# Weight halves split into high and low part by two transfers instead of by ScalarE and VectorE

## The chip, the core and the metric

The kernel runs on one core of one Trainium2 chip. The core has a matrix engine (TensorE, in the profile PE, its weight loads PEld), two elementwise engines (VectorE, in the profile DVE, and ScalarE, in the profile ACT), a third one that also issues transfers (GpSimd, POOL), a queue that only issues transfers (SyncE, SP) and 16 DMA engines that all queues share. The metric is the device time of one execution in microseconds (us), lower is better. A profile of one execution stands beside the timed runs.

## What is computed

One layer of a hybrid encoder block on 512 tokens of width 1024, all in float32: a normed projection into 11520 columns, three token mixers side by side (a gated short convolution, a gated linear recurrence, and a delta-rule recurrence over 16 heads in chunks of 64 tokens), their gated sum, an output projection with residual, and a squared-ReLU MLP with residual and a last norm.

```python
h = rms_norm(x, norm1_g[l])
p = h @ w_in[l]                                   # 1024 x 11520
...
m = gate_a * y_a + gate_b * y_b + gate_c * y_c
x = x + m @ w_out[l]                              # 1024 x 1024
h2 = rms_norm(x, norm2_g[l])
x = x + jnp.square(jax.nn.relu(h2 @ mlp_w1[l])) @ mlp_w2[l]   # 1024 x 4096 x 1024
return rms_norm(x, final_g)
```

## The kernel before

**Split products.** TensorE's fast 32-bit type (float32r) holds fewer bits than float32. So every large operand is split into a high part (the value rounded to float32r) and a low part (the value minus the high part, also float32r), and each product is made of three matmuls, high by high, high by low and low by high (`mm3`, L153 to L155). The activations are split on the chip when they are made (`hh` and `hl`, `h2h` and `h2l`, `ah` and `al`).

**The weight stream.** Weights come in tiles of 128 x 1024, each used for one block of 128 output columns (or, in the second MLP product, 128 rows), and each loaded as two halves of 128 x 512 (256 KB). `load_half` (L127) makes one half: SP loads `raw` (L129, three buffers), ScalarE casts it to `whi` (L131, four buffers), VectorE subtracts to get `wlo` (L94 from L133, four buffers). A tile serves 8 x 3 = 24 matmuls. There are 170 tiles, 340 halves: 180 halves of `w_in`, 32 of `w_out` (each of its 8 tiles is loaded twice, once for each half of the tokens), 64 and 64 of the MLP.

**Stages.** The start loads x, takes its norm (squares by POOL and ScalarE at L232 and L234, their sum by TensorE, the root `rsb` on VectorE at L181) and meanwhile multiplies three tiles with x before its norm's scale; then x is scaled (L251 on POOL for five of the eight parts) and split into `hh` and `hl`. Four groups follow. In each the critical part is the delta-rule recurrence: small matrices (`amat`), a triangular inverse by elimination on VectorE (`dg` and `Z`, 62 steps), and a chain over eight chunks of small matmuls; as filler beside it run the projections of the other mixers, in an order that `weave` and the priorities fix. The output projection (`w_out`) works on half of the tokens at a time, so its matmuls have 256 columns instead of 512. Then the MLP: 32 tiles of `w1`, after each of which ScalarE takes the relu (L914) and splits the square (L922), and 32 of `w2`.

**Order and queues.** A scheduler sets the order of instructions on each engine from the order of the program and priorities; `load_w` asks for priority over what is emitted beside it. Each engine then works strictly in that order: an instruction that waits holds up all behind it, and that is so for queues of transfers too. In this kernel POOL issues some 50 transfers, of intermediate results (`mpd`, `mhd`, `mld`, `mh`, `ml`, `x2d`) and of x; SP issues all weights. POOL's own computing is the four squares and five scalings of the start, a few fills, and eight products at the very end.

Of the kernel before, what the change touches and what calls it, by code (L numbers as in the profile page):

```python
# [9 lines left out]
F32 = mybir.dt.float32  # L10
# [8 lines left out]
P = 128  # L19
# priorities of the weight stream, the prologue and the critical steps over what is emitted beside them  # L20
OFF, OFFS, OFFP = 160, 20, 30
CP, CPI, CPP = 150, 60, 30
# empty steps that leave the latency of an inverse, or of a norm, to the filler
NINV, NPOST = 16, 6
# steps of the fillers, and their shares by part of the critical path
# [63 lines left out]
def block_kernel(ctx, tc, xt, win, par, mulr, sw, wout, w1, w2, fg, cst, eyes, out):  # L89
# [3 lines left out]
    def tt(o, a, b, op):  # L93
        return v.tensor_tensor(out=o, in0=a, in1=b, op=op)  # L94
# [32 lines left out]
    def load_half(src, i):  # L127
        raw = wp.tile([P, S], F32, tag="raw", name="raw", bufs=3)
        sy.dma_start(raw, src[:, i * S:(i + 1) * S])  # L129
        hi = wp.tile([P, S], F32R, tag="whi", name="whi", bufs=4)  # L130
        ac.copy(hi, raw)  # L131
        lo = wp.tile([P, S], F32R, tag="wlo", name="wlo", bufs=4)
        tt(lo, raw, f(hi), SUB)  # L133
        return hi, lo
# [22 lines left out]
    def pin(first, mm):  # L157
        # in the order of the program, behind the matmuls before it
        if first:
            tc.keep_in_program_order(mm)  # L160

    def rsqrt(x, y, t):
        # Newton's steps from a first guess on the exponent; within 2 ulp after the third
# [6 lines left out]
    def rsqrt_rows(pool, o, ps, low, scale=1.0):  # L170
        # rows alike in each 32: tokens to partitions, the root there, and back
# [11 lines left out]
    # =======================================================================  # L183
    # projections and the three branches
    # =======================================================================
# [24 lines left out]
    wlr = [[load_half(win[CN[("lr", 0)]], 0)]]  # L210
    for a, n in ((0, 1), (1, 1), (2, 2)):
        sy.dma_start(xT[:, a:a + n], xt[a:a + n].rearrange("k p t -> p k t"))
    wlr[0].append(load_half(win[CN[("lr", 0)]], 1))
# [81 lines left out]
    # low-rank inputs, and the first key tile, on x before its norm's scale  # L295
# [10 lines left out]
    # derived per-channel values  # L306
    # sigmoid(z) = (1 + tanh(z / 2)) / 2 throughout: tanh shares its table with exp
# [30 lines left out]
    # softplus of the recurrence's parameter  # L338
# [33 lines left out]
    def krv(g, G_):  # L372
# [5 lines left out]
        for jj in range(2):  # L378
# [51 lines left out]
            # by head: the two tiles' halves side by side  # L430
# [17 lines left out]
    def amat(G_):  # L448
        # A^T = [b|k]^T [a|r], masked
# [605 lines left out]
```

## Time and profile before

| | |
|---|---|
| Median of 3 runs | 1188.13 us (1186.85 to 1191.43) |
| Profiled execution, its span | 1188.4 us |
| TensorE busy | 1155.3 us (97%) |
| VectorE busy | 786.9 us (66%) |
| ScalarE busy | 550.5 us (46%) |
| POOL busy | 59.2 us (5%) |
| Moved by DMA | 114.69 MB, mean 97 GB/s |

The profiled execution has no time of its own beside its span; it lies within the three timed runs. The profile gives for each group of instructions the source line, engine, operation, output and inputs, the count, then the busy time and the mean duration of one, and last the idle time of the engine just before them with what ended it. Matmuls overlap, so that the mean duration of one (410 ns) is longer than the distance from one to the next. The line is often that of a helper: all of VectorE's two-operand operations have L94, and the tile's name tells them apart.

### The profile page before, as it was taken

What the parts mean: (1) busy time and instruction counts of PE and PEld (TensorE: products, weight loads), DVE (VectorE), ACT (ScalarE), POOL (GpSimd) and SP (SyncE); (2) the same over time, 40 slices, a digit from 0 to 9 for tenths busy, and PEclk for the clock granted to TensorE, in tenths of its full rate; (3) what the DMA queues carried; (4) which work ended last, traced back from release to release, by engine and by line L of the source; (5) the groups of instructions that cost most, each with busy time, mean ns of one, the idle gap of its engine ahead of it and who ended that gap; (6) DMA issues with size and microseconds to landing.
All of it is one profiled execution on the core that took longest, in us unless ns stands there. A gap on an engine that the chain in (4) does not pass through costs nothing.

```text
span 1188.4 us, 17270 instructions
## 1 busy us (share of the span) xinstructions
PE 1155.3 (97%) x6396; PEld 896.6 (75%) x6396; DVE 786.9 (66%) x1537; ACT 550.5 (46%) x1005; POOL 59.2 (5%) x99
## 2 busy tenths in 40 slices
PE   8999989999999999989999989999999999999996
PEld 4677876677777677767677766889888888888885
DVE  7997985689975678985688975677544444222225
ACT  6655364444556443565444545556444443222224
POOL 4100000000000000000000011000000000000003
PEclk9899988999999999999999999999999999999999
DMA  5231230222332122233122244436323333433322
GB/s 183 89 89 54 89 98 28 63 85 71 96 114 72 41 80 80 85 106 90 46 80 67 71 126 150 151 116 187 124 90 98 89 98 118 154 101 91 105 89 98
DMA packets 61973, 114.69 MB, mean 97 GB/s; under 512 B 7232, under 2 KB 10816, under 8 KB 61888
## 3 DMA queue, kind: packets, MB, share of 16 engines
q1 hardware_dynamic: 54960, 95.49, 26.2%
q0 software_dynamic: 6352, 17.30, 4.6%
q8 instruction: 50, 0.82, 0.3%
q10 hardware_dynamic: 576, 0.79, 0.2%
q14 instruction: 35, 0.29, 0.1%
HBM read 104.64 MB, written 8.91 MB: 96 GB/s over the span
## 4 chain that ended last, share of the span: by engine, by line
PE 84%; DVE 12%; issue 2%; ACT 1%; DMA 0%; SPq 0%; DVEq 0%; ACTq 0%
PE pp L153 12%; PE pp L155 11%; PE pp L154 11%; PE acc L153 6%; PE acc L154 6%; PE acc L155 6%; PE p L155 5%; PE p L153 5%; PE p L154 5%; DVE wlo L94 3%; PE py L582 2%; PE pA L458 2%; PE py L584 2%; DVE Z L94 2%; DVE dg L94 2%
## 5 line engine op out<-in xcount | busy, mean ns | idle before, releaser
L94 DVE TENSOR_TENSOR wlo<-raw,whi 128x512 fp32r<-128x512 f32 x340 | 235.4, 695 | 250.6 <-ACT whi L131 241.7
L131 ACT CAST whi<-raw 128x512 fp32r<-128x512 f32 x340 | 209.7, 619 | 379.1 <-PE acc L155 124.5
L155 PE MATMUL pp<-hh,wlo 128*128 128x512 f32 x696 | 284.4, 410 | 14.8 <-DVE wlo L94 14.5
L153 PE MATMUL pp<-hh,whi 128*128 128x512 f32 x696 | 285.0, 412 | 1.3 <-ACT hh L254 1.3
L154 PE MATMUL pp<-hl,whi 128*128 128x512 f32 x696 | 282.1, 407 | 3.1 <-DVE hl L97 3.1
L155 PEld LDWEIGHTS pp<-hh,wlo 128*128 128x128 f32 x696 | 133.2, 191 | 53.1 <-DVE wlo L94 21.6
L153 PEld LDWEIGHTS pp<-hh,whi 128*128 128x128 f32 x696 | 133.2, 191 | 34.6 <-issue 1.9
L154 PEld LDWEIGHTS pp<-hl,whi 128*128 128x128 f32 x696 | 133.4, 192 | 33.6 <-DVE hl L97 3.7
L155 PE MATMUL p<-h2h,wlo 128*128 128x512 f32 (+1 forms) x264 | 103.0, 390 | 0.1
L153 PE MATMUL p<-h2h,whi 128*128 128x512 f32 (+1 forms) x264 | 103.0, 390 | 0.0
L154 PE MATMUL p<-h2l,whi 128*128 128x512 f32 (+1 forms) x264 | 102.8, 389 | 0.0
L154 PE MATMUL acc<-wlo,ah 128*128 128x512 f32 x256 | 99.7, 390 | 0.0
L155 PE MATMUL acc<-whi,al 128*128 128x512 f32 x256 | 99.6, 389 | 0.0
L153 PE MATMUL acc<-whi,ah 128*128 128x512 f32 x256 | 99.6, 389 | 0.0
L155 PEld LDWEIGHTS p<-h2h,wlo 128*128 128x128 f32 x264 | 49.7, 188 | 11.6 <-DVE wlo L94 0.3
L154 PEld LDWEIGHTS p<-h2l,whi 128*128 128x128 f32 x264 | 49.7, 188 | 11.3
L153 PEld LDWEIGHTS p<-h2h,whi 128*128 128x128 f32 x264 | 49.7, 188 | 11.3
L154 PEld LDWEIGHTS acc<-wlo,ah 128*128 128x128 f32 x256 | 48.1, 188 | 10.1 <-DVE wlo L94 0.3
L153 PEld LDWEIGHTS acc<-whi,ah 128*128 128x128 f32 x256 | 48.1, 188 | 10.1
L155 PEld LDWEIGHTS acc<-whi,al 128*128 128x128 f32 x256 | 48.1, 188 | 10.0
L94 DVE TENSOR_TENSOR Z<-Z,dg 64x31 f32<-64x31 f32 (+15 forms) x124 | 42.2, 340 | 4.1
L94 DVE TENSOR_TENSOR dg<-Z 64x31 f32<-64x31 f32 (+15 forms) x124 | 42.2, 340 | 4.1
(299 smaller groups left out, 1591.3 us busy)
## 6 DMA issues: line engine op xcount, KB each, us to landing
raw<-in_win SPq DMA_DIRECT2D x180, 256.0 KB, 2.6
raw<-in_w SPq DMA_DIRECT2D x128, 256.0 KB, 2.7
raw<-in_wout SPq DMA_DIRECT2D x32, 256.0 KB, 2.6
swr<-in_sw SPq DMA_DIRECT2D x16, 128.0 KB, 2.1
x2T<-in_xt POOLq DMA_DIRECT2D x4, 512.0 KB, 7.1
x2d<-st POOLq DMA_DIRECT2D x8, 256.0 KB, 2.8
xr<-x2d POOLq DMA_DIRECT2D x1, 2048.0 KB, 8.7
xT<-in_xt SPq DMA_DIRECT2D x3, 512.0 KB, 6.8
```

The costliest lines, as they stand in the source:

```text
L94: return v.tensor_tensor(out=o, in0=a, in1=b, op=op)
L131: ac.copy(hi, raw)
L153: pe.matmul(ps, wh, xh, start=start, stop=False)
L154: pe.matmul(ps, wh, xl, start=False, stop=False)
L155: pe.matmul(ps, wl, xh, start=False, stop=stop)
L458: pe.matmul(pts[h][:, ci], G_.BK[rows, jj, c], G_.AR[rows, jj, c], start=True, stop=True)
L582: pe.matmul(o, RT[64 * h:64 * h + 64, jj, c], St[64 * h:64 * h + 64, jj], start=True, stop=False)
L584: pe.matmul(o, AXt[:, 2 * h + jj, c, 1], sv[:, 2 * h + jj], start=St is None, stop=True)
```

## The change

The changed `load_half` has no `raw` tile in the steady stream. POOL issues a transfer from float32 in memory into the float32r tile `whi`, which rounds on the way. ScalarE writes the negated high part into `wlo`. POOL issues a second transfer of the same weights that adds them to what is in `wlo`, so that `wlo` ends as the weight minus its high part. `whi` has six buffers now, `wlo` five. The two halves of the very first tile keep the old way, with `raw` in a buffer of another pool that is free then. Comments were removed from the source; the lines of the changed kernel are shifted by 7, so the matmuls of `mm3` are L160 to L162 there.

```diff
-    def load_half(src, i):
-        raw = wp.tile([P, S], F32, tag="raw", name="raw", bufs=3)
-        sy.dma_start(raw, src[:, i * S:(i + 1) * S])
-        hi = wp.tile([P, S], F32R, tag="whi", name="whi", bufs=4)
-        ac.copy(hi, raw)
-        lo = wp.tile([P, S], F32R, tag="wlo", name="wlo", bufs=4)
-        tt(lo, raw, f(hi), SUB)
+    def load_half(src, i, pool=None):
+
+        src = src[:, i * S:(i + 1) * S]
+        hi = wp.tile([P, S], F32R, tag="whi", name="whi", bufs=6)
+        lo = wp.tile([P, S], F32R, tag="wlo", name="wlo", bufs=5)
+        if pool is not None:
+            raw = pool.tile([P, S], F32, tag=("lgh", "lgl")[i], name="raw")
+            sy.dma_start(raw, src)
+            ac.copy(hi, raw)
+            tt(lo, raw, f(hi), SUB)
+            return hi, lo
+        gp.dma_start(hi, src)
+        ac.activation(lo, f(hi), AF.Copy, scale=-1.0)
+        gp.dma_start(lo, src, accum_op=ADD)
         return hi, lo
...
-    wlr = [[load_half(win[CN[("lr", 0)]], 0)]]
+    wlr = [[load_half(win[CN[("lr", 0)]], 0, sp)]]
...
-    wlr[0].append(load_half(win[CN[("lr", 0)]], 1))
+    wlr[0].append(load_half(win[CN[("lr", 0)]], 1, sp))
```

Three places show what moves. The first is the start on POOL: `sq` are the squares of x for the first norm, `xT` is x. Before:

```order
L232 TENSOR_TENSOR sq<-xT 128x512 [waits DMAHW2_49]
L232 TENSOR_TENSOR sq<-xT 128x512 [waits DMAHW4_49]
L232 TENSOR_TENSOR sq<-xT 128x512 [waits DMAHW6_49]
L925 MEMSET epst 128x1 [waits Activation_49]
L232 TENSOR_TENSOR sq<-xT 128x512 [waits DMAHW7_49]
L251 TENSOR_TENSOR xT<-xT,rsb 128x512 [waits DMAHW3_49,DVE_49,Activation_49]
```

and in the change:

```order
L138 DMA whi<-in_win 128x512 [waits PE_49]
L140 DMA wlo<-in_win 128x512 [waits Activation_49] x2
L138 DMA whi<-in_win 128x512 [waits PE_49]
L140 DMA wlo<-in_win 128x512 [waits DMASW0_49,Activation_49]
L140 DMA wlo<-in_win 128x512 [waits DMASW1_49,Activation_49]
L140 DMA wlo<-in_win 128x512 [waits DMASW2_49,Activation_49]
L239 TENSOR_TENSOR sq<-xT 128x512 [waits DMAHW7_49]
```

The fourth square, which waited for nothing but x, now stands behind six transfers of `whi` and five of `wlo`, two of the former waiting for TensorE (PE) and all of the latter for ScalarE (Activation).

The second place is the first MLP product. Before, SP's queue held the loads of `raw` and nothing else, here of `w_out` and the MLP:

```order
L129 DMA raw<-in_wout 128x512 x32
L129 DMA raw<-in_w 128x512 x128
```

In the change POOL's queue has, with the buffers' numbers (a `wlo` has the number of its `whi` plus one):

```order
L138 DMA whi_8668<-in_w1 128x512
L140 DMA wlo_8634<-in_w1 128x512
L138 DMA whi_8673<-in_w1 128x512
L140 DMA wlo_8669<-in_w1 128x512
L138 DMA whi_8708<-in_w1 128x512
L140 DMA wlo_8674<-in_w1 128x512
L138 DMA whi_8713<-in_w1 128x512
```

The adding transfer of half 8668 stands behind the casting transfer of the next half, 8673, and ahead of that of the one after, 8708.

The third place is the second pass of the output projection, again on POOL in the change; before, POOL had only the stores of `x2d` there:

```order
L865 DMA x2d<-st 128x512 x8
```

and now:

```order
L138 DMA whi_7485<-in_wout 128x512
L140 DMA wlo_7415<-in_wout 128x512
L140 DMA wlo_7448<-in_wout 128x512
L140 DMA wlo_7453<-in_wout 128x512
L138 DMA whi_7490<-in_wout 128x512
L140 DMA wlo_7486<-in_wout 128x512
L138 DMA whi_7523<-in_wout 128x512
L872 DMA x2d_69<-st_7374 128x512
L138 DMA whi_7528<-in_wout 128x512
L140 DMA wlo_7491<-in_wout 128x512
L138 DMA whi_7561<-in_wout 128x512
L140 DMA wlo_7524<-in_wout 128x512
```

Here the adding transfer of half 7490 stands behind the casting transfers of the next two, 7523 and 7528, and a store of `x2d` stands between.

## The prediction

> **What bounds the kernel now.** I read the page first (busy time, chain of waits, costliest groups), then the stretches, then the timelines of single engines. The page:
>
> ```profile
> PE 1155.3 (97%) x6396; PEld 896.6 (75%) x6396; DVE 786.9 (66%) x1537; ACT 550.5 (46%) x1005; POOL 59.2 (5%) x99
> ...
> PE 84%; DVE 12%; issue 2%; ACT 1%; DMA 0%; SPq 0%; DVEq 0%; ACTq 0%
> ...
> L94 DVE TENSOR_TENSOR wlo<-raw,whi 128x512 fp32r<-128x512 f32 x340 | 235.4, 695 | 250.6 <-ACT whi L131 241.7
> L131 ACT CAST whi<-raw 128x512 fp32r<-128x512 f32 x340 | 209.7, 619 | 379.1 <-PE acc L155 124.5
> L155 PE MATMUL pp<-hh,wlo 128*128 128x512 f32 x696 | 284.4, 410 | 14.8 <-DVE wlo L94 14.5
> ```
>
> TensorE is the bound: 97% busy, 33 us idle in 1188.4. VectorE's low parts cost 235 us of VectorE but only 14.5 us of TensorE's idle time. In stretches (columns: PE, PEld, DVE, ACT, POOL busy, clock, DMA share, GB/s):
>
> ```profile
> 0.00:50.00 50.00, 41.59 (x136) 27.55 (x136) 41.15 (x76) 31.49 (x53) 16.26 (x22) 0.93 0.45 141
> 600.00:700.00 100.00, 95.16 (x448) 73.97 (x445) 88.40 (x165) 44.07 (x74) 4.31 (x8) 0.98 0.27 83
> 900.00:1000.00 100.00, 100.00 (x429) 80.38 (x428) 47.43 (x71) 42.12 (x72) 0.00 (x0) 1.00 0.30 95
> 1100.00:1188.00 88.00, 78.88 (x348) 64.81 (x346) 30.69 (x48) 25.86 (x50) 9.26 (x7) 0.98 0.29 96
> ```
>
> Of the 33 us, 8.4 lie in the start and 9.1 in the last stretch, which the change does not reach; what VectorE could give back is the 14.5. VectorE is the bound only inside the elimination of each group; for the last one, all engines and then the wlo instructions alone:
>
> ```profile
> 645.00:692.00 47.00, 45.53 (x193) 35.54 (x192) 43.97 (x95) 21.41 (x35) 0.64 (x2) 1.00 0.26 78
> 645.00:692.00 47.00, 9.00 (x13) 1.00 0.26 78
> ```
>
> VectorE has 44 of 47 us there, 9 of them for wlo, but TensorE is at 45.5 of 47 on filler: a shorter elimination moves TensorE's work and removes little of it. TensorE's own pace, from its timeline:
>
> ```profile
> 662.14 0.40 PE L153 MATMUL pp<-hh,whi 128*128 128x512 f32 x1
> ...
> 671.98 0.40 PE L153 MATMUL pp<-hh,whi 128*128 128x512 f32 x1
> ```
>
> These are 14 rounds of three matmuls in 9.84 us: 0.234 us each. A weight tile has 24 of them, 5.63 us, so a half (256 KB) is used up every 2.81 us in the MLP and under dense filler.
>
> **The change part by part.** It removes 338 of 340 subtractions from VectorE (338 x 0.695 = 235 us). ScalarE exchanges a cast for a negation of the same shape, about 0.62 us both. SP's weight loads go to POOL, twice: 338 casting and 338 adding transfers, 676 issues. The nearest rows are a plain POOL load of 256 KB (its issue, then its landing), a run of ten such loads, and SP's load:
>
> ```profile
> L717 POOL DMA_DIRECT2D u<-mpd x6: 544/546/562, 314.7 to 728.3; - x6
> DMA to landing us min/median/max: 2.9/3.7/4.5
> ...
> DMA to landing us min/median/max: 2.9/4.8/6.0
> raw<-in_w SPq DMA_DIRECT2D x128, 256.0 KB, 2.7
> ```
>
> Issuing alone is 676 x 0.55 = 372 us of POOL, which has 59 busy: hidden. In engine time, the MLP row (share 0.30 at 95 GB/s) puts the full rate at 317 GB/s, so 256 KB cost 0.83 us. No row shows a cast or an add. I take the casting load at 0.83; the adding one lies between 0.83 (as a load) and 1.66 (a load plus a second reading of the same size). A pair is then 1.66 to 2.49 us, below 2.81: by bytes the MLP still fits.
>
> The Trainium skill speaks against the change here: "Collectives: The Full Stack", section "The bandwidth ceiling: the fold count and why AG ≠ RS ≠ AR", says that an adding DMA step runs at about half the rate of a copy, since it has to read two sources through one read ring. By that rule the adding transfer is at the upper end, 1.66 us; the terms below would be 31 us for the MLP and 22 for the output projection, and the sum 1241. No row of this trace can show it.
>
> The tighter limit is **a loop through POOL's queue**. As the order of instructions shows, whi of half n is issued, then wlo of n-1, then whi of n+1, then wlo of n; and wlo of n waits for ScalarE's negation, which waits for whi of n to land. Behind that waiting issue stands whi of n+2. So two halves take one loop: landing 3.7 + negation 0.62 + issue 0.55, and some queueing, because the previous adding transfer, issued 0.55 earlier, is ahead in the same queue (the ten loads in a row landed after 2.9 at the least, 6.0 at the most). That is 1.66 - 0.55 = 1.11 at the upper end, 0.28 with a plain load, 0.70 halfway; I take 0.83, one plain transfer, since the landings of 3.7 were had with less than half of the traffic. The loop is 5.70 us, against TensorE's 5.63 for two halves. Lower end 2.9 + 0.62 + 0.55 = 4.07, upper end 4.5 + 1.11 + 0.62 + 0.55 = 6.78.
>
> *MLP, 64 tiles.* In the second product (32 tiles) the loop misses by 0.07 x 32 = 2 us. In the first, ScalarE is also held for each tile:
>
> ```profile
> 892.52 0.59 ACT L914 ACTIVATE r<-p 128x512 f32<-128x512 f32 x1
> 893.98 0.62 ACT L922 CAST ah<-r 128x512 fp32r<-128x512 f32 x1 [0.86 <-DVE r L94]
> ```
>
> From 892.52 to 894.60 it is 2.1 of 5.63 us; a landing that falls into it (0.37 of the time) waits 1.05 on average, so 0.39 more, and (0.07 + 0.39) x 32 = 15 us. From a slot's release TensorE has five halves, 14.1 us, and the way to a landed low part takes the 5.70 and another landing, 3.7 + 0.83, 10.2 in all, so 3.9 us are in reserve: 2 + 15 - 4 = **+13**. Ends: 0 (loop at 4.07) and (6.78 - 5.63) x 64 + 12 = +86.
>
> *Output projection.* Its matmuls have half the width, so halves go fast (casts to whi, columns as before):
>
> ```profile
> 790.00:800.00 10.00, 3.63 (x7) 1.00 0.57 161
> 800.00:810.00 10.00, 2.78 (x5) 1.00 0.65 205
> 810.00:820.00 10.00, 4.31 (x7) 1.00 0.62 191
> 820.00:830.00 10.00, 3.70 (x6) 1.00 0.58 167
> ```
>
> 25 halves in 40 us, 1.6 us each, with the DMA at 0.6 already for one load per half. In the new order three whi run ahead there, so the loop gives 5.70 / 3 = 1.90, and the pair's engine time 1.66 to 2.49. I take 2.1: 25 x 0.5 = **+12**. Ends: +1 (1.66) and +22 (2.49).
>
> *Groups.* 13 halves in 47 us are 3.6 us each, and the loop gives 2.85, so the stream keeps up there and no longer waits for VectorE. Of the 14.5 us I take two thirds back: **-10**. Ends: -14.5 and 0 (ScalarE's and POOL's own waits take VectorE's place).
>
> *Start.* POOL squares four x tiles for the first norm; the fourth now stands behind six whi, two of which wait for TensorE to be done with the first tile's halves, and five wlo, which wait for ScalarE:
>
> ```profile
> 11.48 1.45 POOL L232 TENSOR_TENSOR sq<-xT 128x512 f32<-128x512 f32 x1
> ...
> 23.18 0.71 DVE L181 STREAM_TRANSPOSE rsb<-rqq 128x512 f32<-128x512 f32 x1
> 24.02 8.02 POOL L251 TENSOR_TENSOR xT<-xT,rsb 128x512 f32<-128x512 f32 x5 [11.10 <-ACT spt L343]
> ```
>
> I estimate the fourth at 20 instead of 11.5, and rsb, the norm's scale, some 8 us later; 48 matmuls on unscaled x (11.3 us) cover part. **+5**; ends 0 (all covered) and +10 (nothing covered, and POOL's five scalings interrupted by issues).
>
> *Other work in POOL's queue.* Ten loads of mh and ml and one of mab were alone there:
>
> ```profile
> 710.58 0.54 POOL L799 DMA_DIRECT2D mh<-mhd  x1 [11.93 <-ACT AXt L521]
> ...
> 716.24 0.72 POOL L801 DMA_DIRECT2D mab<-mpd  x1 [0.34 <-DMA mh<-mhd]
> ```
>
> Now weights stand behind the 6.4 us of issues and their 3.1 MB (9.9 us at 317 GB/s), against 3.9 in reserve: **+5**; ends 0 (TensorE's small matmuls of the chain cover it) and +12 (the wait for AXt counts too).
>
> Sum against the profiled execution: 1188.4 - 10 + 5 + 5 + 12 + 13 = 1213. The median run, 1188.13, is the same within 0.3. All lower ends together: 1188.4 - 14.5 + 1 = 1175; all upper ends: 1188.4 + 10 + 12 + 22 + 86 = 1318.
>
> **The rivals.** *Everything is hidden* (chance 0.21): whi lands near 2.9, the loop is 4.07, six slots of whi and five of wlo cover the rest, and the 14.5 us come back less a little at the start: 1176. For it: 11.2 to 14.1 us of lead. Against it: median POOL landings of 3.7 with less than half of the traffic. *The transfers are slow* (0.17): casting or adding costs the engines more than a row shows; it decides once a pair takes over 2.81 us. At 3.3: 128 x 0.49 = 63 in the MLP, 25 x 1.7 = 42 in the projection, and the 10 of the start and mh: about 1303. At 4.0: 152 + 60 + 10 and 4 x 13 x 0.4 = 21 in the eliminations: 1431. For it: no row shows such a transfer; against it: nothing either. *Loss and gain cancel* (0.12): loop at 5.2, the projection at 1.8, 1185 to 1192. That the subtraction does not leave VectorE is excluded by the order.
>
> **How the numbers follow.** About 0.5% (6 us) is what a measurement of this kernel can tell from no change. The forecast, 1195 to about 1265, has 0.50; faster 0.21; same 0.12; slower 0.50 + 0.17 = 0.67. The range of 8 in 10 goes from 1174, just under the hidden case, to 1325, which leaves out the worse half of the slow transfers. The forecast's own range is 1195 to 1265.
>
> **What would show it.** Right: POOL near 370 us of issues or above; VectorE down by 235; POOL waiting for ScalarE's wlo in the MLP; TensorE idle before L162 with a DMA as releaser from 790 to 830 and in the MLP; the weight transfers landing at 3.7 to 5 us. The fourth squaring near 20 us would bear out the start. Wrong: no idle time of TensorE in the MLP (hidden case), or DMA shares near 1 with landings over 8 us (slow transfers). If POOL's issue takes over 1.4 us, POOL itself sets the pace, and the loop was the wrong step.

## The result and the profile after

The changed kernel takes 1354.24 us, median of four runs (1349.96 to 1369.02), against 1187.49 us (1185.57 to 1191.43) for the kernel before: a ratio of 1.142, 95% interval 1.137 to 1.146. It is 14% slower. The forecast was 1213, its range 1174 to 1325: the direction was right, the size was not.

Three kinds of rows of the page after (busy time; chain of waits; costliest groups):

```profile
PE 1210.9 (89%) x6396; PEld 918.9 (68%) x6396; DVE 581.0 (43%) x1199; ACT 549.9 (41%) x1005; POOL 536.4 (40%) x775
...
issue 32%; PE 31%; POOL 21%; DMA 10%; ACT 3%; DVE 3%; POOLq 0%; SPq 0%; ACTq 0%; DVEq 0%
...
L139 ACT ACTIVATE wlo<-whi 128x512 fp32r<-128x512 f32 x338 | 212.6, 630 | 547.6 <-DMA whi<-in_w 192.0
...
L140 POOL DMA_DIRECT2D wlo<-in_w x128 | 110.3, 865 | 222.3 <-ACT wlo L139 212.9
...
L161 PE MATMUL acc<-wlo,ah 128*128 128x512 f32 x256 | 105.6, 413 | 30.8 <-DMA wlo<-in_w 30.7
```

VectorE's 235 us of low parts are gone, and its busy time is shorter by 206 us (581.0 instead of 786.9; some of those rows overlapped others). TensorE has fallen from 97 to 89% busy, although its busy time has grown from 1155.3 to 1210.9 us with the same 6396 matmuls. The chain that was 84% TensorE is now TensorE, POOL, DMA and issue. The third to fifth row give its links in order: ScalarE's negation waits for the casting transfer, POOL's adding transfer waits for the negation, TensorE waits for the adding transfer. No engine is the bound; a sequence of latencies is.

The same in stretches (columns: PE, PEld, DVE, ACT, POOL busy, clock, DMA share, GB/s):

```profile
0.00:50.00 50.00, 37.36 (x119) 25.00 (x120) 38.02 (x74) 27.81 (x46) 29.06 (x43) 0.93 0.78 182
600.00:700.00 100.00, 95.78 (x595) 69.22 (x596) 65.81 (x153) 41.59 (x86) 28.41 (x42) 1.00 0.53 106
900.00:1000.00 100.00, 88.92 (x413) 69.93 (x414) 21.56 (x36) 36.04 (x67) 47.29 (x69) 0.97 0.86 181
1200.00:1300.00 100.00, 88.67 (x367) 68.70 (x366) 0.00 (x0) 19.09 (x31) 42.46 (x60) 0.98 0.81 159
```

In the two stretches of the MLP (the last two rows) TensorE is busy for 88.9 and 88.7 of 100 us; before, it had 100 of 100 from 900 to 1000. Where each stage ends is read from the first and last start of the matmuls that only it has, `mh,whi` (output projection), `h2h,whi` (first MLP product), `whi,ah` (second). Before, then after:

```profile
L153 PE MATMUL acc<-mh,whi x128: 274/281/390, 757.2 to 822.0; 128*128 128x256 f32 x128
L153 PE MATMUL p<-h2h,whi x264: 277/397/483, 822.3 to 1003.7; 128*128 128x512 f32 x124, 128*128 128x256 f32 x8
L153 PE MATMUL acc<-whi,ah x256: 387/389/393, 1004.4 to 1178.0; 128*128 128x512 f32 x128
```

```profile
L160 PE MATMUL acc<-mh,whi x128: 274/282/583, 814.2 to 918.5; 128*128 128x256 f32 x128
L160 PE MATMUL p<-h2h,whi x264: 277/394/628, 911.4 to 1122.0; 128*128 128x512 f32 x124, 128*128 128x256 f32 x8
L160 PE MATMUL acc<-whi,ah x256: 387/389/632, 1122.7 to 1342.0; 128*128 128x512 f32 x128
```

The table has the same three ends for every kernel of this study, as durations in us of the profiled execution. The stages overlap a little, and an execution can differ from the median by some us, so differences under 5 us are not read. The median leaves out executions over 1.5% above the kernel's fastest: two of "every second half" (1341.5, the profiled one, and 1344.9) and one of its "groups only" (1284.5). The expectations were written with other marks for the stages (430 us for the MLP after, where the table has 423.5, and 97 for the output projection, where it has 104.3).

| kernel | to the end of the output projection | of it, to its first matmul | MLP 1 | MLP 2 | rest | median of the runs |
|---|---|---|---|---|---|---|
| before | 822.0 | 757.2 | 181.7 | 174.3 | 10.4 | 1187.5 |
| after | 918.5 | 814.2 | 203.5 | 220.0 | 12.9 | 1354.2 |
| more high buffers (7 and 4) | 860.8 | 769.9 | 185.6 | 194.9 | 12.6 | 1256.7 |
| casting alone | 863.9 | 784.0 | 182.0 | 180.9 | 12.7 | 1243.2 |
| adding alone | 874.4 | 786.4 | 186.6 | 206.3 | 11.9 | 1281.4 |
| loop cut | 824.7 | 741.0 | 181.1 | 180.2 | 13.0 | 1202.2 |
| no adding | 854.8 | 771.0 | 181.1 | 175.4 | 13.9 | 1234.1 |
| 7 and 5 buffers | 843.0 | 754.6 | 184.8 | 213.8 | 13.2 | 1259.3 |
| negated twice | 941.8 | 844.2 | 221.9 | 243.0 | 12.5 | 1429.8 |
| every second half | 922.3 | 826.3 | 195.3 | 210.8 | 11.4 | 1330.3 |
| every second half, groups only | 885.7 | 804.6 | 181.8 | 174.2 | 10.2 | 1258.1 |
| GpSimd subtracts | 851.5 | 782.2 | 182.3 | 174.3 | 10.3 | 1224.1 |
| three castings ahead | 855.3 | 768.3 | 184.4 | 184.0 | 13.0 | 1228.1 |
| three ahead, groups only | 835.3 | 753.5 | 182.3 | 175.8 | 10.6 | 1207.2 |

Of the 166.5 us between the two profiled executions, 96.5 are lost by the end of the output projection, 21.8 in the first and 45.7 in the second MLP product.

Part of this is a price that none of the edits below isolates: TensorE's granted clock. The traces show it at 1 or at 0.5; at 1 a 512-column matmul starts every 234 ns, at 0.5 every 427 ns (medians in the kernel after). Up to the end of the output projection, before and then after, followed by two stretches of that projection in the kernel after (columns as above):

```profile
0.00:822.00 822.00, 798.44 (x4818) 604.91 (x4819) 640.75 (x1314) 422.55 (x780) 46.53 (x86) 0.98 0.30 92
```

```profile
0.00:918.50 918.50, 830.17 (x4830) 628.62 (x4831) 521.07 (x1105) 423.55 (x784) 346.25 (x513) 0.94 0.69 143
819.00:842.00 23.00, 23.00 (x122) 17.84 (x120) 5.95 (x19) 6.11 (x16) 6.57 (x10) 0.50 0.68 158
845.00:868.00 23.00, 19.26 (x162) 16.39 (x162) 9.72 (x31) 8.17 (x19) 11.19 (x16) 1.00 0.79 162
```

At half clock TensorE was busy all the time and made 122 matmuls in 23 us; at full clock it made 162, with idle time between them. Up to the end of the output projection its idle time grew from 24 to 88 us and its time at half clock from 31 to 102 us. Half of the latter growth, 36 us, is the most that it can have cost; the two together, 65 + 36, cover the 96.5. Over the whole execution idle time grew by 111 us and time at half clock by 92, so up to 46 of the 166.5 us are the clock's. An estimate from the spans and mean clocks says the same: span times clock is 1289 to 1297 us in the four executions after and 1169 to 1175 before, some 120 us apart.

In the kernel after, each of the 17 stretches at half clock begins when TensorE has been idle for at least 1.3 of the 3.4 us before it; in other runs some begin without any idle time, so what sets them off is not shown. With the loop cut the clock is 0.989 again (0.985 before, 0.953 after), so this price goes with the turn; but casting alone, which has no turn, also shows 0.970. Where a run below is compared, the time at half clock is given where it is a large part of the loss.

The turn can be seen on POOL and on ScalarE in the second MLP product of the kernel after (timelines: start, duration, what, idle time before it and its releaser):

```profile
1230.63 0.84 POOL L140 DMA_DIRECT2D wlo<-in_w  x1 [4.22 <-ACT wlo L139]
1231.17 0.87 POOL L138 DMA_DIRECT2D whi<-in_w  x1
1232.52 0.85 POOL L140 DMA_DIRECT2D wlo<-in_w  x1 [0.48 <-ACT wlo L139]
1233.07 0.88 POOL L138 DMA_DIRECT2D whi<-in_w  x1
1237.27 0.85 POOL L140 DMA_DIRECT2D wlo<-in_w  x1 [3.33 <-ACT wlo L139]
...
1244.14 0.85 POOL L140 DMA_DIRECT2D wlo<-in_w  x1 [3.30 <-ACT wlo L139]
```

```profile
1236.34 0.63 ACT L139 ACTIVATE wlo<-whi 128x512 fp32r<-128x512 f32 x1 [4.11 <-DMA wlo<-in_w]
```

The high part issued at 1231.17 is negated at 1236.34, and the adding transfer that needs this goes out at 1237.27; behind it stands the next casting transfer. From one such adding transfer to the next it takes 6.64 us (1230.63 to 1237.27) and 6.87 (to 1244.14), for the two halves of one weight. The stage's mean is 220.0 / 32 = 6.88. TensorE could use them up in 5.45 (174.3 / 32, before; in the first product 181.7 / 32 = 5.68). (The releaser named on ScalarE's row, a landing of `wlo`, is long past by the order of the issues; the wait is for the casting transfer.)

### The profile page after: what moved, and what is told of

It is laid out like the page before. It is cut to its first block, busy times and chain, and to the rows that moved or that the text cites. A ratio compares the mean times of both kernels' runs of the same rounds, so it can differ in the third digit from the quotient of the medians.

```text
span 1354.9 us, 17282 instructions
## 1 busy us (share of the span) xinstructions
PE 1210.9 (89%) x6396; PEld 918.9 (68%) x6396; DVE 581.0 (43%) x1199; ACT 549.9 (41%) x1005; POOL 536.4 (40%) x775
## 4 chain that ended last, share of the span: by engine, by line
issue 32%; PE 31%; POOL 21%; DMA 10%; ACT 3%; DVE 3%; POOLq 0%; SPq 0%; ACTq 0%; DVEq 0%
POOL whi L138 12%; POOL wlo L140 9%; PE pp L162 6%; PE pp L161 5%; PE pp L160 5%; DMA whi<-in_win 4%; DMA wlo<-in_w 2%; PE py L589 2%; PE py L591 2%; DMA wlo<-in_win 1%; PE pu L557 1%; PE pT L524 1%; ACT wlo L139 1%; PE pS L574 1%; PE pu L565 1%
## 5 line engine op out<-in xcount | busy, mean ns | idle before, releaser
L139 ACT ACTIVATE wlo<-whi 128x512 fp32r<-128x512 f32 x338 | 212.6, 630 | 547.6 <-DMA whi<-in_w 192.0
L162 PE MATMUL pp<-hh,wlo 128*128 128x512 f32 x696 | 287.9, 415 | 17.8 <-DMA wlo<-in_win 17.8
L160 PE MATMUL pp<-hh,whi 128*128 128x512 f32 x696 | 283.6, 409 | 4.1 <-ACT hh L261 4.1
L140 POOL DMA_DIRECT2D wlo<-in_win x178 | 155.7, 883 | 235.2 <-ACT wlo L139 230.7
L138 POOL DMA_DIRECT2D whi<-in_win x178 | 128.4, 726 | 211.0 <-PE pp L162 143.7
L140 POOL DMA_DIRECT2D wlo<-in_w x128 | 110.3, 865 | 222.3 <-ACT wlo L139 212.9
L162 PEld LDWEIGHTS pp<-hh,wlo 128*128 128x128 f32 x696 | 133.6, 192 | 56.2 <-DMA wlo<-in_win 25.7
L160 PEld LDWEIGHTS pp<-hh,whi 128*128 128x128 f32 x696 | 134.2, 193 | 35.4 <-ACT hh L261 4.6
L161 PE MATMUL acc<-wlo,ah 128*128 128x512 f32 x256 | 105.6, 413 | 30.8 <-DMA wlo<-in_w 30.7
L162 PE MATMUL p<-h2h,wlo 128*128 128x512 f32 (+1 forms) x264 | 107.5, 408 | 12.7 <-DMA wlo<-in_w 12.1
L138 POOL DMA_DIRECT2D whi<-in_w x128 | 107.8, 847 | 9.4 <-PE acc L162 5.0
L160 PE MATMUL p<-h2h,whi 128*128 128x512 f32 (+1 forms) x264 | 103.4, 392 | 0.1
L162 PE MATMUL acc<-whi,al 128*128 128x512 f32 x256 | 102.1, 400 | 0.0
L160 PE MATMUL acc<-whi,ah 128*128 128x512 f32 x256 | 101.7, 398 | 0.0
L97 DVE SCALAR_TENSOR_TENSOR xr<-acc,sc,xr 128x512 f32<-128x512 f32 x8 | 6.0, 745 | 202.0 <-PE acc L162 202.0
L94 DVE TENSOR_TENSOR r<-r 128x512 f32<-128x512 f32 x32 | 22.2, 692 | 131.2 <-ACT r L921 131.2
L162 PEld LDWEIGHTS p<-h2h,wlo 128*128 128x128 f32 x264 | 49.9, 189 | 39.0 <-DMA wlo<-in_w 29.5
L161 PEld LDWEIGHTS p<-h2l,whi 128*128 128x128 f32 x264 | 50.1, 190 | 11.4
```

Source lines behind the costliest of these rows:

```text
L138: gp.dma_start(hi, src)
L139: ac.activation(lo, f(hi), AF.Copy, scale=-1.0)
L140: gp.dma_start(lo, src, accum_op=ADD)
L160: pe.matmul(ps, wh, xh, start=start, stop=False)
L161: pe.matmul(ps, wh, xl, start=False, stop=False)
L162: pe.matmul(ps, wl, xh, start=False, stop=stop)
```

## The experiments

Two theories stood against each other. **Loop**: what costs is the turn through POOL's queue (casting transfer lands, ScalarE negates, adding transfer goes out, next casting transfer goes out), which takes longer than TensorE takes for the halves it covers. **Bytes**: what costs is that two transfers for each half, one of them adding, fill the DMA engines. A third question came up on the way: what is left when the loop is gone.

### What a transfer costs by itself

A kernel that only moves weights: 40 plain loads of 256 KB each from SP and POOL, 40 casting ones, 40 adding ones without and 40 with a cast, then eight of each of POOL's kinds one at a time.

```diff
+    for k in range(N):                      # casting loads
+        gp.dma_start(T[k], src(k))
+    for k in range(N):                      # adding and casting
+        gp.dma_start(T[k], src(k), accum_op=add)
```

> All of the block's work is left out: 40 loads of 256 KB back to back on SP (plain), then on POOL 40 plain, 40 casting, 40 adding without a cast and 40 adding with a cast, each into 40 separate tiles, then 8 of each POOL kind into one tile, each waiting for the one before. It prices the disputed transfers by themselves. Theory L (the loop through POOL's queue: landing, negation, issue, two halves for each turn, sets the pace of the changed kernel; the engines have room): plain and casting near 0.8 us each in a row, adding at most 1.7, so a pair under 2.5 us against TensorE's 2.81 a half; one at a time a casting load lands after about 3 us. Theory D (the 16 DMA engines set the pace): casting plus adding take 3.2 us or more of the engines, as much as the 3.3 to 3.4 us a half that the MLP of the changed kernel needs.

The rate in 40 equal slices of its 316 us; then the casting and the adding transfers one at a time, each with its landing:

```profile
GB/s 221 389 388 386 389 385 389 279 387 388 383 205 205 205 204 205 204 204 243 262 211 204 204 206 153 99 67 71 95 66 82 60 62 63 66 66 66 66 66 66
```

```profile
L111 POOL DMA_DIRECT2D t<-in_w x8: 527/529/536, 219.7 to 243.2; - x8
...
DMA to landing us min/median/max: 2.8/3.1/3.3
```

```profile
L115 POOL DMA_DIRECT2D t<-in_w x8: 857/861/865, 279.5 to 308.3; - x8
...
DMA to landing us min/median/max: 3.7/3.8/4.1
```

Plain and casting loads run at the same 387 GB/s, 0.68 us for 256 KB: the cast costs the engines nothing. Adding transfers run at 205 GB/s, 1.28 us, with and without a cast. A pair is 1.95 us, well under the 2.81 us that TensorE takes for a half.

A second such kernel asks whether the prices add up when the two kinds alternate in one queue, and when compute engines work beside them.

> The block's work is left out. Four stretches of 256 KB transfers from the weights on POOL's queue: 20 plain casting ones; then 60 pairs of a casting and an adding transfer in turn, to tiles of their own; the same 60 pairs beside TensorE (8 matmuls a pair), ScalarE and VectorE; then 40 casting ones beside TensorE. Alone and unmixed the two kinds took 0.68 and 1.28 us of the DMA engines. If prices add up, a pair takes 1.95 us, 268 GB/s, in both stretches of pairs. If mixing two kinds in one queue costs (the theory of slow transfers), the first stretch of pairs shows 2.4 us or more (under 220 GB/s); if it is the engines' work that slows the transfers, only the second does.

```profile
GB/s 185 357 315 253 267 272 274 270 269 271 274 264 269 273 273 265 271 272 272 271 269 299 280 272 273 271 269 272 272 258 274 273 268 270 274 376 384 383 394 78
...
q0 software_dynamic: 43200, 78.66, 111.8%
```

Throughout the stretches of pairs it runs at some 271 GB/s, 1.94 us for a pair. The matmuls, which wait for nothing, fill only the first half of the span, so it is the first half of these slices that stands beside the engines; its rate is no lower. The prices add up. The second row is a warning for the reading of traces: the packets of one queue took 111.8% of the 16 engines' span, so packets overlap in this share and in the DMA columns. A share near 1 does not mean that no more could be moved.

### The loop cut, its bytes kept

```diff
-        ac.activation(lo, f(hi), AF.Copy, scale=-1.0)
+        ac.activation(lo, wcon, AF.Copy, scale=-1.0)
```

> The changed kernel, with one thing else: ScalarE's negation reads a constant tile in place of the high part, so that it no longer waits for the casting transfer (the low parts are then the whole weights, so the product is another; instructions, bytes and buffers are those of the changed kernel). Loop through POOL's queue: the turn is gone, MLP 360 to 385 us in place of 430, in all 1190 to 1250. Transfers fill the DMA engines: the MLP stays above 410 and the whole above 1310.

1202.19 us, ratio 1.013 (1.009 to 1.016): 152 of the 167 us are gone with one operand. Bytes, transfers, buffers and queues are the same. In POOL's order one or two castings now stand ahead of an adding transfer instead of two; the negation, and with it the adding transfer, no longer waits for them. Its page, POOL's timeline in the second MLP product, and a stretch of the first:

```profile
PE 1157.0 (97%) x6396; PEld 897.7 (75%) x6396; DVE 582.8 (49%) x1200; ACT 549.1 (46%) x1005; POOL 540.0 (45%) x775
```

```profile
1125.10 0.55 POOL L141 DMA_DIRECT2D whi<-in_w  x1 [2.52 <-PE acc L165]
...
1130.54 0.55 POOL L141 DMA_DIRECT2D whi<-in_w  x1 [2.52 <-PE acc L165]
```

```profile
900.00:1000.00 100.00, 100.00 (x429) 80.39 (x428) 24.93 (x36) 42.58 (x72) 50.64 (x72) 1.00 0.97 187
```

POOL now waits for TensorE to free a slot, and the rows come every 5.44 us: TensorE sets the pace again. The DMA share is 0.97 with TensorE at 100 of 100, more than the 0.86 of the kernel after. The theory of bytes falls here. Of the 152 us, up to 50 are time at half clock that went with the turn (129 us of it after, 30 here). Against the kernel before, the end of the output projection is 2.7 us late and the MLP 5 us. Its first matmul comes 16.2 us earlier than before, but up to 12 of these are the clock too: 7 us at half clock up to there, against 31.

### The turn made longer by a known time

```diff
         ac.activation(lo, f(hi), AF.Copy, scale=-1.0)
+        ac.activation(lo, f(hi), AF.Copy, scale=-1.0)
```

> The changed kernel with ScalarE negating each half twice (the second time over the first), 0.63 us more in every turn of POOL's queue and nothing else on it; ScalarE was busy 41% of the span. Loop: with turns of 6.6 to 6.9 us for two halves in the MLP, 64 turns there become 40 us longer, MLP 465 to 475 in place of 430; over all 169 turns at most 106 us, so 1400 to 1460 in all. Had the transfers' bytes set the time, 0.63 us of a ScalarE that has room would move it by less than 10 us: 1345 to 1365.

1429.84 us, ratio 1.201 (1.191 to 1.211), 76 us more than the change. The MLP went from 423.5 to 464.9 us, 41.4 more, where 64 turns of 0.63 give 40.3. POOL's adding transfers in the second product:

```profile
1294.43 0.86 POOL L141 DMA_DIRECT2D wlo<-in_w  x1 [4.92 <-ACT wlo L140]
...
1302.35 0.86 POOL L141 DMA_DIRECT2D wlo<-in_w  x1 [5.04 <-ACT wlo L140]
...
1309.79 0.86 POOL L141 DMA_DIRECT2D wlo<-in_w  x1 [4.57 <-ACT wlo L140]
```

7.92 and 7.44 us; the stage's mean is 243.0 / 32 = 7.59, 0.72 more than the 6.88 of the kernel after. What is added to the turn appears in the MLP's time. By products it is 18.4 us, 0.57 for each turn, in the first, where POOL's order is that of the kernel after, and 23.0 us, 0.72 each, in the second, where two and three castings stand ahead in turn. Before the MLP, 23.3 us were lost over 105 turns, 0.22 each: by this the turn would bind about a third of the time there, which one pair of profiles is too coarse to show.

### The turn made shorter by a cheaper neighbour

The second transfer casts without adding: it still waits for the negation, and only its engine time falls from 1.28 to 0.68 us.

```diff
-        gp.dma_start(lo, src, accum_op=ADD)
+        gp.dma_start(lo, src)
```

> The changed kernel, with the second transfer casting without adding (the low parts are then copies of the high ones; it still waits for the negation, so queue, loop and buffers stay, and only the engine time of a pair falls from 1.95 to 1.36 us). Loop: the turn is shorter only by what the casting transfer lands earlier, 0.5 to 1.0 us of 6.7, so MLP 375 to 410 and in all 1270 to 1325. Transfers fill the DMA engines: MLP under 370, in all under 1250.

1234.05 us, ratio 1.039 (1.025 to 1.053). Landings (count, KB each, median us from issue to landing), of the kernel after and of this one:

```profile
whi<-in_w POOLq DMA_DIRECT2D x128, 256.0 KB, 4.9
wlo<-in_w POOLq DMA_DIRECT2D x128, 256.0 KB, 4.3
```

```profile
whi<-in_w POOLq DMA_DIRECT2D x128, 256.0 KB, 3.4
```

The MLP came out at 356.5 us against 356.0 before: hidden. This is better than the loop's expectation (375 to 410) and by its numbers alone looks like the theory of bytes; with the run before, which kept all the bytes and got the time back too, it reads otherwise. The casting transfer is itself unchanged. It lands 1.5 us earlier with no adding transfer in front of it; that would bring the turn from 6.88 to about 5.4, no longer than TensorE's 5.45. I had put this shortening at 0.5 to 1.0 us. Bytes matter, but as latency within the turn.

### Buffers, and who is ahead of whom in POOL's queue

The order of instructions shows how many casting transfers are issued before an adding one waits for the first of them. In the change it is two nearly everywhere. With seven high and four low buffers it is mostly four (four and three in turn in the second MLP product), with seven and five mostly three, without any other edit.

```diff
-        hi = wp.tile([P, S], F32R, tag="whi", name="whi", bufs=6)
-        lo = wp.tile([P, S], F32R, tag="wlo", name="wlo", bufs=5)
+        hi = wp.tile([P, S], F32R, tag="whi", name="whi", bufs=7)
+        lo = wp.tile([P, S], F32R, tag="wlo", name="wlo", bufs=4)
```

> The changed kernel with seven buffers for whi and four for wlo instead of six and five, the same space. On POOL four casting transfers now stand ahead of the adding transfer of the first of them instead of two, so one turn of the loop serves four halves; bytes and transfers are the same. Theory L: a turn of 6.7 us gives 1.7 us a half, below 2.81, so the MLP (431 us in the changed kernel, 356 before) goes back to 360 to 380, the output projection (97 us, 65 before) to 75 to 85, and the whole to 1210 to 1260. Theory D: nothing changes by more than 2%, 1330 to 1375, DMA share in the MLP still 0.8.

1256.72 us, ratio 1.059 (1.056 to 1.062): 98 us back with the same bytes. The MLP took 380.5 us, at the upper edge of what the loop's side gave and not near the 356 of before: with four low buffers the negation now waits for TensorE to free one.

With seven and five:

> The changed kernel with seven buffers for high parts and five for low ones (six and five in the change, seven and four in the first experiment, which took 1256.7 with 387 us in the MLP). If what is left there is the low part's landing against four buffers (negation waits for TensorE's release, the adding transfer lands 5.1 us later), the MLP falls to 358 to 372 and the whole to 1215 to 1240. If it is the engine time of the pairs, it stays at 380 to 390 and 1245 to 1260.

1259.28 us, ratio 1.061 (1.055 to 1.066): no better, which in the total is what the engine time of the pairs was to give (1245 to 1260); but the MLP, 398.6 us, lies above both expectations. Its two products say something else: 184.8 us (before: 181.7) and 213.8 (before: 174.3). In the first, three castings stand ahead throughout; in the second, two and three in turn. POOL's adding transfers in the first product, then in the second:

```profile
905.89 0.85 POOL L140 DMA_DIRECT2D wlo<-in_w  x1 [0.36 <-ACT wlo L139]
...
908.71 0.87 POOL L140 DMA_DIRECT2D wlo<-in_w  x1 [0.36 <-ACT wlo L139]
```

```profile
1106.73 0.86 POOL L140 DMA_DIRECT2D wlo<-in_w  x1 [4.96 <-ACT wlo L139]
...
1113.39 0.86 POOL L140 DMA_DIRECT2D wlo<-in_w  x1 [3.79 <-ACT wlo L139]
```

One half every 2.82 us and hardly a wait, against a turn of 6.66 us for two. Same buffers, same bytes, another order. So the order was edited alone, by a priority for the casting transfers that leaves three or four ahead everywhere:

```diff
-        gp.dma_start(hi, src)
+        with tc.high_priority(offset=200):
+            gp.dma_start(hi, src)
```

> The changed kernel with seven and five buffers, as in the run that took 1259, and one thing else: the casting transfers have a priority of their own, so that three or more castings stand ahead of each adding transfer in POOL's order in every stage (there: three in the groups and the first MLP stage, two and three in turn in the second). If the castings ahead decide, the second MLP stage goes from 213 to 174 to 182 us as the first one did, and the whole to 1200 to 1230, near the run without the loop (1202). If the buffers or the bytes decide, it stays at 1250 to 1262.

1228.05 us, ratio 1.034 (1.030 to 1.038), 31 less than without the edit, inside the loop's range. The second product fell from 213.8 to 184.0 us; its adding transfers now go out in pairs, every 5.4 to 5.9 us:

```profile
1156.84 1.78 POOL L141 DMA_DIRECT2D wlo<-in_w  x2
...
1162.76 1.78 POOL L141 DMA_DIRECT2D wlo<-in_w  x2
...
1168.19 1.78 POOL L141 DMA_DIRECT2D wlo<-in_w  x2
```

With this, 126 of the change's 167 us are taken back with all of the change in place. What is left is 41 us by the medians; of the 48 in the profiled execution, 33 stand before the end of the output projection, up to 17 of them time at half clock (65 us against 31), and 12 in the MLP.

### Every second half by the new way

Only the first half of each weight comes by the new way; the second by SP, ScalarE and VectorE as before.

```diff
+        if pool is None and (i == 1):
+            pool = wp
```

> The new way for the first half of each weight, the old one (SyncE's load, ScalarE's copy, VectorE's subtraction) for the second; raw 2, high 5, low 4 buffers. One casting, negation and adding per weight: a turn of 5.2 to 6.5 us has TensorE's 5.63 us for a whole weight to hide in. Loop: the MLP within 15 us of before (356), the groups keep 5 to 12 us of VectorE's relief: 1170 to 1205. If POOL's queue costs also without a turn that binds (start, output projection), 1205 to 1230.

1330.3 us, ratio 1.117 (1.108 to 1.127). That is above both expectations, 100 us above the nearer, and the kernel with half of the adding transfers is only 24 us faster than the one with all. In a group and in the MLP:

```profile
380.13 0.87 POOL L142 DMA_DIRECT2D wlo<-in_win  x1 [4.29 <-ACT wlo L141]
...
386.36 0.86 POOL L142 DMA_DIRECT2D wlo<-in_win  x1 [4.81 <-ACT wlo L141]
```

```profile
1121.22 0.87 POOL L142 DMA_DIRECT2D wlo<-in_w  x1 [4.47 <-ACT wlo L141]
...
1127.78 0.88 POOL L142 DMA_DIRECT2D wlo<-in_w  x1 [4.38 <-ACT wlo L141]
```

These turns take 6.2 and 6.6 us and each gives one half of the new kind, that is, one weight: about what the two halves of a weight took with two castings ahead. The order has one casting ahead here, since there is one such half for each weight. A turn has its length whether it carries one half or two; what counts is how many stand ahead. I had expected 5.2 to 6.5 us and weighed it as hidden; 210.8 / 32 = 6.59 is not. Of the 100 us lost by the end of the output projection, 50 are idle time of TensorE and up to 55 are the clock's (140 us at half clock against 31).

The same, for the groups' projections alone:

> The same halves, but only for the projections of the groups; start, output projection and MLP load as before. If VectorE's relief is worth what the run without the loop showed in the groups (16 us for all of the weights, with the start's loss in it), a half of it is 5 to 12 us: 1175 to 1184, faster by 0.5 to 1%. If the turn still binds in the bursts of projections, 1188 to 1200.

1258.1 us, ratio 1.059 (1.052 to 1.065). The MLP is as before (181.8 and 174.2), and the whole loss, 64 us, stands before its begin: 33 are idle time of TensorE and up to 24 the clock's (78 us at half clock against 31). So the turn binds in the groups too, which the expectation had put at 12 us at most.

### The parts alone

Against the kernel before: casting alone (raw tiles and VectorE's subtraction kept), then adding alone (raw tiles and ScalarE's cast kept). The two halves of the first tile stay as they were in both.

```diff
-        ac.copy(hi, raw)
+        gp.dma_start(hi, src[:, i * S:(i + 1) * S])
```

> The kernel before with one part of the change alone: whi comes from a casting transfer on POOL, while raw still comes over SP and VectorE still subtracts. Two transfers a half, none of them adding, and no transfer on POOL waits for ScalarE, so there is no loop. Theory L: 1185 to 1200, since POOL's queue only waits for TensorE's release of a slot. Theory D in the form that the bytes cost: two loads a half, 1.7 us of engine time in 2.81, some loss in the output projection, 1190 to 1215; if casting itself is slow, over 1230.

```diff
-        tt(lo, raw, f(hi), SUB)
+        ac.activation(lo, f(hi), AF.Copy, scale=-1.0)
+        gp.dma_start(lo, src[:, i * S:(i + 1) * S], accum_op=ADD)
```

> The kernel before with the other part alone: raw over SP, ScalarE casts it to whi and then writes the negated whi to wlo, POOL's transfer adds the weights. The adding transfer waits for ScalarE, but no casting transfer stands behind it. ScalarE has 338 more operations of 0.63 us. Theory L: 1180 to 1215, the MLP at 356 to 365. Theory D: the adding transfer's engine time stays, so the MLP is still above 400 us and the whole over 1260.

1243.22 us, ratio 1.047 (1.044 to 1.051), and 1281.39, ratio 1.079 (1.076 to 1.083): both outside what the loop gave for them (1185 to 1200, 1180 to 1215), and by their totals where the theory of bytes had them (over 1230 if casting is slow, over 1260). Against that reading stand the price of a casting transfer, which is that of a plain one, and the MLP of adding alone, 392.9 us where over 400 were foreseen. Casting alone has no turn in which POOL waits for another engine's answer; its MLP is near that of before (+7 us), but 42 us are lost by the end of the output projection, up to 17 of them the clock's (65 us at half clock against 31). Each of its four high buffers, once free, now stands empty for a landing instead of for ScalarE's 0.62 us; that this is the cause is argued, no run takes it apart. In adding alone POOL waits 750.9 us for ScalarE's negation, and the low part of a half comes a cast, a negation and a landing after its buffers are free, with four buffers; it loses 32 us in the second product alone.

### Is VectorE's relief worth anything?

Two runs give VectorE less to do at no price in the MLP. GpSimd in VectorE's place for every second low part, in the kernel before:

```diff
+        if i == 1:
+            gp.tensor_tensor(out=lo, in0=raw, in1=f(hi), op=SUB)
+        else:
+            tt(lo, raw, f(hi), SUB)
```

> The kernel before, with GpSimd in VectorE's place for the subtraction of every second half: no transfer added, no loop, about 120 us off VectorE. By the 2.02 us that a 128x512 product took on GpSimd at the start it has 5.63 us for one a weight. If the groups' gain is VectorE's relief alone, 1172 to 1184. If GpSimd's subtraction lands late or disturbs VectorE, 1187 to 1210.

1224.09 us, ratio 1.030 (1.025 to 1.035), worse than either side had it. The loss, 30 us, is all before the MLP. A small operation of the elimination, of the kernel before (the kernel after has the same 42.2 and 340) and of this one (busy time, mean ns of one):

```profile
L94 DVE TENSOR_TENSOR Z<-Z,dg 64x31 f32<-64x31 f32 (+15 forms) x124 | 42.2, 340 | 4.1
```

```profile
L94 DVE TENSOR_TENSOR Z<-Z,dg 64x31 f32<-64x31 f32 (+15 forms) x124 | 55.6, 448 | 4.1
```

GpSimd's elementwise work makes VectorE's operations longer, 340 to 448 ns in the mean, in the very stage that was to be relieved. The Trainium skill says so: in "SBUF — State Buffer", section "SBUF: two separate sides", the two engines share one pair of ports and hold it exclusively. The trace agrees that they disturb each other.

And the new way with three castings ahead, for the groups' projections alone, the rest as before:

> The new way with three castings ahead only for the projections of the groups; start, output projection and MLP load as in the kernel before, with raw tiles in the ring of the seven high buffers. If VectorE's relief is a gain once the turn is hidden, the groups end 5 to 16 us earlier than before (757): 1170 to 1183, faster by 0.4 to 1.4%. If the low parts' landing or POOL's other work eats it, 1184 to 1200.

1207.17 us, ratio 1.017 (1.013 to 1.020), above both expectations. The output projection's first matmul comes 3.7 us earlier than before, with the same 31 us at half clock, its end 13.3 us later, and the MLP is within 2 us. VectorE's busy time is 685 us, 102 less than before. What that is worth in the groups is about 4 us: 3.7 here, and 16.2 less up to 12 for the clock in the run without the loop. Nothing among these runs beats the kernel before, and the run without the loop, which I take for about the best that an order could reach (argued, not shown), does not either (1.009 at the lower end of its interval).

## Why the prediction was right and where it was wrong

**Right: the mechanism.** The prediction named the loop through POOL's queue as the tighter limit and the bytes as fitting. Cutting the loop gives 152 of 167 us back, a pair costs 1.95 us of the engines (1.66 to 2.49 foreseen, bound 2.81; the full rate is 387 GB/s, not the 317 read from the rows), and the rows to look for were there: POOL's issues above 370 us, VectorE's low parts gone (206 us off its busy time, not 235), POOL waiting for `wlo` of ScalarE, TensorE waiting at a DMA in the MLP, weight transfers landing at 4.3 to 5.5 us. The fourth squaring was foreseen near 20 us:

```profile
21.38 2.02 POOL L239 TENSOR_TENSOR sq<-xT 128x512 f32<-128x512 f32 x1
```

**Wrong: the size of the turn.** The prediction had landing 3.7, queueing 0.83, negation 0.62, issue 0.55: 5.70 us, 0.07 over TensorE's pace. The row chain of the result has 0.54 for the issue of the adding transfer, 5.17 from the casting issue to the negation, 0.63, and 0.30 until the next issue: 6.64. So landing and queueing are 5.17 in place of 4.53, and the hand-over from ScalarE to POOL, 0.30, had no term at all. Because the turn stood so near to TensorE's pace, an error of 0.94 us in 5.70 makes the MLP's loss: (6.64 - 5.63) x 64 = 65 us, measured 67.5 in place of +13. That the sum fits so closely is partly luck. The products lost 21.8 and 45.7 us, not 32 each: their mean turns were 6.36 and 6.88, and TensorE's own pace before was 5.68 in the first and 5.45 in the second, where the prediction used 5.63 for both. The prediction's upper end for the turn, 6.78, was where it came out; the middle was taken for the forecast, although it lay 1% from TensorE's pace. One row was read too kindly: the longest landing of 6.0 is that of the five `mh` loads, and the `ml` loads beside them, counted among the ten, took up to 6.7.

The Trainium skill, in "Collectives: The Full Stack", section "The bandwidth ceiling: the fold count and why AG ≠ RS ≠ AR", puts a reduce step at about half the rate of a copy step. This case's adding transfer agrees: 205 against 387 GB/s, a factor of 0.53. The prediction's sum by that rule (1241) was nearer, but still far from 1354.

**Wrong: the groups.** This is the step that failed most. Up to the output projection's first matmul, where start, groups and POOL's other work lie, the terms add up to 0 (-10 + 5 + 5), and 57.0 us were measured: TensorE's idle time grew by 46 us there and its time at half clock by 38, for which no term stood. The prediction took -10 for the groups, from 13 halves in 47 us of the elimination, 3.6 us each, against a loop that "gives 2.85". Two things are wrong in it. The mean hides that the projections come in bursts at TensorE's full pace, one half in 2.81 us; the run with the turns in the groups alone lost 64 us before the MLP, and the one without the loop ends the output projection where the kernel before does. And the turn is longer there, in part because ScalarE's negations stand in line behind its other work (in the burst shown next, those at 314.01, 317.56, 322.68 and 331.53 start with no idle time of ScalarE before them). Adding transfers of the kernel after in a burst, the first and the last of 13:

```profile
300.58 0.86 POOL L140 DMA_DIRECT2D wlo<-in_win  x1 [0.86 <-ACT wlo L139]
...
344.69 0.88 POOL L140 DMA_DIRECT2D wlo<-in_win  x1 [3.88 <-ACT wlo L139]
```

Twelve steps in 44.1 us are 3.68 us a half, not 2.85. Start, groups, POOL's other work and output projection together were put at -10 + 5 + 5 + 12 = +12; 96.5 were measured. Without the loop they are +2.7: apart from the turn, these terms were about right in sum, with some luck, since that run has 17 us at half clock up to there and the kernel before 31.

**Wrong: the output projection,** +12 with a loop of 5.70 / 3. By the order, two to four castings stand ahead there, most often two; its own duration went from 64.8 to 104.3 us, 83.7 without the loop. So some 20 us go with the turn, up to 12 of them the clock's (34 us at half clock against 10), and 19 remain without it, part of which is only that the stage begins earlier (741.0 instead of 757.2).

**The rivals.** Slow transfers are excluded (1.95 us for a pair, and the time comes back with all the bytes in place). Hidden and cancelled are excluded by the result. What the range lacked was not a rival but a term: its upper end added +10 for the start, +12 for POOL's other work and 0 for the groups, so the turn was allowed to bind only from the output projection on, and a lower clock nowhere.

**Open.** What lowers the clock is open, and with it how much of the loss before the MLP is waiting and how much is slower matmuls; 36 us are the most for the latter. A casting transfer lands after 3.1 us alone, 3.4 beside its own kind and 4.9 here. What stands ahead of it in the queue explains up to 0.74 us (an adding transfer of 1.28, issued 0.54 earlier); the rest, about 1 us, is not explained by prices that add up. VectorE is no part of it: it is idle in the second product (0.00 busy from 1200 to 1300), where landings are as long. Nor is it settled why some 14 us stay at the output projection when only the groups take the new way.

## What to carry to other kernels

Where a queue issues a transfer, waits for an engine's answer to it and only then issues the next, work out the whole turn with every hand-over and compare it with the consumer's pace in its densest stretch, not with a mean. Here a turn forecast 1% above that pace came out 16% longer than forecast, so a turn that near should be counted as binding. Such a turn is hidden by work that stands ahead of the waiting instruction in that queue (here three castings instead of two), which is a matter of order; more buffers helped here where they changed that order. A second transfer in place of a short operation on an engine with 34% idle time bought nothing here; ask first whether the critical stage waits for that engine. And compare TensorE's busy time and granted clock before and after: 55.6 us more for the same matmuls were a loss that no wait shows.

## What was not expected of the hardware

A cast from float32 to float32r on the way costs the DMA engines nothing (387 GB/s for plain and for casting loads), while adding takes 1.9 times as long (205 GB/s), and its issue, one at a time, keeps POOL's row for 0.86 us instead of 0.53. The DMA share is no measure of what is left: 0.97 in a stretch where TensorE lost nothing, and 111.8% for a queue that moved 271 GB/s. Halving the number of adding transfers took only 24 us off the full change's time; the number of turns had stayed the same. TensorE's granted clock is either 1 or 0.5 in these traces, and the kernel after spent 129 us at 0.5, the kernel before 37.
